# A decoder layer on one core: the normalized rows of the residual are made in the last pair's slot and kept in DRAM

## The chip, the cores and the metric

The kernel runs on one core of a Trainium2 chip. A core has five engines with a queue each: TensorE (PE) for matmuls, VectorE (DVE) and ScalarE (ACT) for elementwise work, GpSimd (POOL), and SyncE (SP), which here issues nearly all DMA transfers. PE writes its results to PSUM; everything else lies in SBUF, and the weights, the input and some scratch tensors lie in DRAM. Each engine works through its own instructions in an order that is fixed when the kernel is built. The metric is the time of the program on the device in microseconds.

## The reference

A hybrid decoder layer in float32, with 512 tokens, 16 learned meta tokens in front of them, and a width of 1024. Sliding-window attention and an RWKV-7 time mixing read the same normalized input, and their gated sum is projected and added to that same normalized input:

```python
h = layer_norm(jnp.concatenate([meta, x], axis=1), ln0_g, ln0_b)
proj = h @ w_in[l]
# q, k, v, zr, gate_att, gate_rwkv are cut out of proj
att = lax.map(lambda qkv: swa_one(...), (q, k, v))
rw = rwkv7_time_mix(zr, ...)
merged = jax.nn.sigmoid(gate_att) * att + jax.nn.sigmoid(gate_rwkv) * rw
h = layer_norm(ALPHA * h + merged @ w_out[l], ln1_g[l], ln1_b[l])
ff = jnp.square(jax.nn.relu(h @ w_ff1[l])) @ w_ff2[l]
h = layer_norm(ALPHA * h + ff, ln2_g[l], ln2_b[l])
```

The change concerns the `h` in `ALPHA * h + merged @ w_out[l]`: token rows of the input, normalized with `ln0_g` and `ln0_b`.

## The kernel before

**Precision.** Every float32 matmul is made of three matmuls of rounded parts: high by high, high by low, low by high. Each weight tile is therefore loaded (L268), cast to its high part on ACT (L258) and subtracted to its low part on DVE (L261). The tiles `wraw`, `whi` and `wlo` rotate in two to three buffers.

**Start.** The four blocks of 128 token rows are loaded, their mean and inverse deviation are computed and kept for the whole kernel in `moments0`, and the normalized rows are transposed to `hhi` and `hlo` (channels by tokens). The token rows themselves are not kept: their memory is given to the next stage.

**Pairs.** The 16 heads are worked on in 8 pairs, in slots. A slot weaves two things into PE's order: dense units (24 matmuls each with weights from `w_in`, later the output projection with `w_out`), and short steps of the attention and of the RWKV scan at given times within the slot. `weave` takes steps of a unit until the time of the next item is reached, then issues that item. This hand-written order holds for PE alone. The orders of DVE, ACT, POOL and SP come from a planner that starts what is ready by rank; `with ahead(n)` raises the rank of the instructions in it by n places, and a negative n lowers it.

In the last slot (`s == PAIRS`, about 563 to 604 us) the scan of pair 7 is solved: triangular blocks, folds (L866 on DVE to `WT`, L884 on DVE to `AX`), a chain of seven dependent steps (L937 on PE, then L895 on DVE and L897 on ACT, each writing half of `Z`), then outputs and a group norm. The dense units of this slot are the first three quarters of the output projection: L1244 to L1246, in four units of (half of the columns n, two token blocks), three quarters q of the input channels each. By then the sum of pairs 0 to 5 has come back from DRAM to the tiles `mf` in the buffers "u", "L", "tw", "ta", "Px", "rk" and was split to `hhi` and `hlo` by `merged` (L1211 on ACT, L1212 on DVE).

**Join.** After the slot the pools of the pairs are closed, and pools for the rest are opened in their memory. `res` holds the four blocks of token rows (128 x 1024 each). The rows are loaded again from `x` (L1443), and `ln0_g` and `ln0_b` are broadcast to 128 partitions (L1434, 512 KB each). Block 3 is normalized in four POOL passes (L1451); blocks 0, 1 and 2 in two DVE passes each (`norm_rows`, L1438 and L1439). Meanwhile PE does the last quarter of the output projection, block by block: twelve matmuls each. `first_norm(b)` then adds the projection to `res[b]` (L1501), takes statistics (L1482), normalizes (L1506, with L226 on POOL for the inverse root), turns the block on PE (L1512, eight transposes), applies `ln1_g` and `ln1_b` on ACT (L1515), and splits it to `h1hi` (L1520, ACT) and `h1lo` (L1521, DVE). The planner, not the hand-written order, places these instructions on PE.

**Feed-forward.** `up` (L331 to L333) multiplies by `w_ff1`, squares the positive part, and `project` multiplies by `w_ff2`. The first three tiles of `w_ff1` are applied to the first 256 tokens (blocks 0 and 1) before the other 256, so that PE can begin before blocks 2 and 3 are ready.

Of the kernel before, what the change touches and what calls it, by code (L numbers as in the profile page):

```python
# [11 lines left out]
F32 = mybir.dt.float32  # L12
# [3 lines left out]
ALU = mybir.AluOpType  # L16
# [4 lines left out]
P = 128  # L21
D = 1024
KT = D // P
SEQ = 512
# [6 lines left out]
NCH = SEQ // C  # L31
# [36 lines left out]
ROW0 = {}  # L68
# [11 lines left out]
SBB = 2  # L80
# [4 lines left out]
NBUF = {'AX': 2, 'BK': 1, 'NT': 2, 'GR': 2, 'Z': 8}  # L85
# [46 lines left out]
def hybrid_layer_kernel(ctx: ExitStack, tc: tile.TileContext, I: dict, out: bass.AP):  # L132
    nc = tc.nc
    dve, act, pool, pe = nc.vector, nc.scalar, nc.gpsimd, nc.tensor
# [8 lines left out]
    dr = ctx.enter_context(tc.tile_pool(name="dr", bufs=1, space=DRAM))  # L143

    @contextmanager
    def ahead(n):

        now = tc.cur_priority
        tc.cur_priority = now - n
        yield  # L150
        tc.cur_priority += n
# [22 lines left out]
    rows = xp.tile([NCOLS, P], F32, name="rows")  # L174
# [54 lines left out]
    def normalize(src, n, tag, on_act):  # L229

        st = xp.tile([P, 2, 6], F32, name="st" + tag)
        for q in range(2):
            dve.bn_stats(st[:n, q, :], src[:n, q * 512 : (q + 1) * 512])
        mv = cst.tile([P, 2], F32, name="mv" + tag)
        dve.bn_aggr(mv[:n], st[:n].rearrange("p a b -> p (a b)"))
        r = rstd_of(cst, mv, n, LN_EPS, tag)
        if on_act:
            nm = xp.tile([P, 2], F32, name="nm" + tag)
            dve.tensor_scalar(nm[:n, 0:1], mv[:n, 0:1], -1.0, None, op0=ALU.mult)
            act.activation(nm[:n, 1:2], nm[:n, 0:1], AF.Copy, scale=r[:n])  # L240
            act.activation(src[:n], src[:n], AF.Identity, bias=nm[:n, 1:2], scale=r[:n])
        else:
            dve.tensor_scalar(
                src[:n], src[:n], mv[:n, 0:1], r[:n], op0=ALU.subtract, op1=ALU.mult
            )
        return mv[:, 0:1], r

    moments0 = [normalize(xt[b], P, str(b), b < 2) for b in range(4)]
# [120 lines left out]
    def step():  # L369

        name, gen = units[0]
        t = next(gen, None)
        if t is None:
            units.pop(0)
            finished.add(name)
            return 0.0
        return t

    def weave(items, rest):


        t = 0.0
        for at_, need, what in sorted(items, key=lambda i: i[0]):
            while units and (t < at_ or not set(need) <= finished):
                t += step()
            assert set(need) <= finished
            what()
        while rest and units:
            step()
# [5 lines left out]
    at = p2.enter_context(tc.tile_pool(name="at", bufs=1))  # L395
    pew = ctx.enter_context(ExitStack())
    ew = pew.enter_context(tc.tile_pool(name="ew", bufs=1))
# [595 lines left out]
    A = {}  # L993
# [225 lines left out]
            nc.sync.dma_start(A["m", j], md[j])  # L1219


    acc = {}
    wout = {}
    bank = {}
    for n, pools in enumerate((((dn, "dn"), (pat, "a")), ((pg, "g"), (pch, None)))):
        for b in range(4):
            pool_, tag = pools[b // 2]
# [102 lines left out]
    F = partial  # L1330

    def scan(j):

        need = (f"k{j}", f"r{j}", f"v{j}")
        return [
            (0.0, need, F(rwkv_scores, j, 0)),
            (3.2, (), F(rwkv_meta, j)),
            (3.2, (), F(rwkv_scores, j, 1)),
            (3.2, (), F(rwkv_inverse, j)),
            (5.6, (), F(rwkv_bonus, j)),  # L1340
            (12.4, (), F(rwkv_turn_scores, j)),
            (19.0, (), F(rwkv_turn_keys, j)),
            (16.0, (), F(rwkv_inverse_place, j)),
            (21.4, (), F(rwkv_turn_values, j)),
        ]

    def solve(j):

        return [
            (0.0, (), F(rwkv_blocks, j, 0)),  # L1350
            (0.0, (), F(rwkv_start, j, 0)),
            (1.4, (), F(rwkv_blocks, j, 1)),
            (1.4, (), F(rwkv_start, j, 1)),
            (3.2, (), F(rwkv_blocks, j, 2)),
            (3.2, (), F(rwkv_start, j, 2)),
            (4.6, (), F(rwkv_blocks, j, 3)),
            (6.4, (), F(rwkv_turn_inverse, j)),
            (8.4, (), F(rwkv_fold, j, 0)),
            (10.6, (), F(rwkv_fold, j, 1)),
        ] + [(11.6 + 0.95 * c, (), F(rwkv_chain, j, c)) for c in range(NCH - 1)] + [  # L1360
            (18.6, (), F(rwkv_outputs, j)),
            (24.5, (), F(rwkv_norm, j)),
        ]

    def project_in(j):
        return [
            (0.0, (), F(rwkv_begin, j)),
            (5.6, (), F(rwkv_lora, j, 0)),
            (7.4, (), F(rwkv_lora, j, 1)),
            (20.4, (f"k{j}",), F(rwkv_sums, j)),  # L1370
        ]
# [13 lines left out]
    def join(j, t2):  # L1385
        return [(t2, (f"gr{j}",), F(merge, j))]

    with tc.manual_schedule(engines={mybir.EngineType.PE}):
        for s in range(-1, PAIRS + 1):
            if s <= PAIRS:  # L1390
                units[:] = [u for u in all_units[: marks[s + 1]] if u[0] not in finished]
            items = []
            if s > 0:
                items += solve(s - 1)
            if 0 <= s < PAIRS:
                items += scan(s)
            if s == -1:
                items += [
                    (0.0, (), F(rwkv_begin, 0)),
                    (9.0, ("wa",), F(rwkv_lora, 0, 0)),  # L1400
                    (10.4, (), F(rwkv_lora, 0, 1)),
                    (20.0, ("k0",), F(rwkv_sums, 0)),
                ]
            if 0 <= s < PAIRS - 1:
                items += project_in(s + 1)
            if s == 0:
                items += [(18.0, ("av",), F(aside_heads, 0))]
            if s == 4:
                items += [(26.0, (), F(aside_heads, 1))]
            if s in (1, 5):  # L1410
                items += [(8.6, (), turn_heads)]
            if 0 < s < PAIRS - 1:
                items += attend(s - 1) + join(s - 1, 31.5)
            if s == PAIRS - 1:
                items += [(10.0, (), merged_before)]
                items += attend(s - 1, t1=20.5) + join(s - 1, 26.5)
                items += attend(s, 16.5)[:4]
                items += [(27.2, (), F(load_out, q, 0)) for q in range(3)]
            if s == PAIRS:
                items += attend(s - 1, t1=1.0)[4:] + join(s - 1, 25.5)  # L1420
                items += [(2.0, (), F(merged, s - 2)), (25.6, (), F(merged, s - 1))]
            weave(items, True)
    pew.close()
    p2.close()
# [5 lines left out]

    def rowvec(name, pool_=rp, tag=None):
        t = pool_.tile([P, D], F32, name="rv" + name, tag=tag or "rv" + name[-1], bufs=WB[2] if tag else 1)
        src = I["rows"][ROW0[name] : ROW0[name] + KT].rearrange("(a r) p -> a (r p)", a=1)
        nc.sync.dma_start(t, src.to_broadcast([P, D]))  # L1434
        return t

    def norm_rows(t, mean, r, g_, b_):
        dve.scalar_tensor_tensor(t, t, mean, g_, op0=ALU.subtract, op1=ALU.mult)  # L1438
        dve.scalar_tensor_tensor(t, t, r, b_, op0=ALU.mult, op1=ALU.add)  # L1439

    res = [rp.tile([P, D], F32, name=f"res{b}") for b in range(4)]
    for b in range(4):
        nc.sync.dma_start(res[b], I["x"][b * P : (b + 1) * P, :])  # L1443
    g0, b0 = rowvec("ln0_g"), rowvec("ln0_b")

    mean, r = moments0[3]
    for op, t in zip(
        (ALU.subtract, ALU.mult, ALU.mult, ALU.add),
        (mean.to_broadcast([P, D]), g0, r.to_broadcast([P, D]), b0),
    ):  # L1450
        pool.tensor_tensor(res[3], res[3], t, op=op)  # L1451

    def project(k0, nk, xhi, xlo, n, hold=2, more=None):

# [68 lines left out]
            )  # L1523

    for b in range(4):
        if b < 2:
            norm_rows(res[b], *moments0[b], g0, b0)
        for n in range(2):
            for d in range(2):
                project_out(KT // 2 - 1, n, b, d)  # L1530
        if 0 < b <= NORMED:
            with ahead(400):
                first_norm(b - 1)
    norm_rows(res[2], *moments0[2], g0, b0)
    pps.close()
    pa = ctx.enter_context(tc.tile_pool(name="pa", bufs=1, space=PSUM))
    ffp = ctx.enter_context(tc.tile_pool(name="ffp", bufs=1))
# [10 lines left out]
    for half in range(2):  # L1548
# [34 lines left out]
        for f in range(split_f, NF):  # L1583
            up(f, load("w_ff1", half * NF + f), 0, SEQ, pb)
            if half == 0 and f in (6, 10):

                row = rowvec(("ln1_g", "ln1_b")[f // 10], wst, "wraw")
                for b in range(4):
                    dve.tensor_tensor(res[b], res[b], row, op=(ALU.mult, ALU.add)[f // 10])
        if half == 0:  # L1590
            g2, b2 = rowvec("ln2_g"), rowvec("ln2_b")
            st2 = stats_tiles()
        for n in range(2):
            ns = slice(n * 512, (n + 1) * 512)
            acc = project(half * NF, NF, fhi, flo, n, HOLD if half and n else 2, ffp)
            for b in range(4):
                dve.scalar_tensor_tensor(
                    res[b][:, ns], res[b][:, ns], 1.0 if half else ALPHA, acc[b],
                    op0=ALU.mult, op1=ALU.add,
# [58 lines left out]
```

## Time and profile before

| | |
|---|---|
| median of 3 runs | 1010.41 us (1008.91 to 1010.78) |
| the profiled execution | 1007.33 us |
| its span, first to last instruction | 1005.4 us |
| mean granted clock of TensorE | 0.985 |
| busy: PE, DVE, ACT, POOL | 948.8, 657.7, 469.9, 55.2 us |
| DMA | 101.26 MB, mean 101 GB/s |

The rows shown below are of one execution. Times within it count from the first instruction. In a row of the timeline the columns are start, length, engine, line, operation, output and inputs, shapes, count; in brackets stands how long the engine had been idle before it, and behind the arrow what ended that. Consecutive instructions of one kind are merged, with their count. In a row that groups instructions, the three numbers behind the count are the shortest, middle and longest duration in ns. "L331" is line 331 of the kernel; weights tiles of all stages go through the same lines L258, L261 and L268.

### The profile page before, as it was taken

Reading aid. Unit: us, or ns where it says so; the run is one execution under the profiler, and the core shown is the slowest. Engines: PE = TensorE matmul, PEld = TensorE weight load, DVE = VectorE, ACT = ScalarE, POOL = GpSimd, SP = SyncE. Lnnn points to the kernel's source line nnn. Section 1 sums busy time; section 2 is a strip of 40 time slices with the busy share of each in tenths; the row PEclk is TensorE's granted clock in tenths of the full one; section 3 lists DMA queues with packets and bytes.
Section 4 is the critical chain, followed back from the end, with each engine's and each line's share of the span. In section 5 each row is a group of like instructions: output and inputs, shape, how many; then the busy total and the mean of one; then the engine's idle time right before and its main releaser. Section 6 shows DMA issues by size and latency. Waiting matters only on the chain.

```text
span 1005.4 us, 19165 instructions
## 1 busy us (share of the span) xinstructions
PE 948.8 (94%) x7533; PEld 792.4 (79%) x7533; DVE 657.7 (65%) x1493; ACT 469.9 (47%) x1238; POOL 55.2 (5%) x112
## 2 busy tenths in 40 slices
PE   4999899999999999999999998699999999999996
PEld 3989688787888878888777676688888888888885
DVE  8678687887886878878786548866432234443436
ACT  6536457574574655845537622644332223432220
POOL 2000000010000100001000004100000000000001
PEclk9999999999999999999999999799999999999999
DMA  7454433224333333242433114323322333232232
GB/s 267 93 148 117 94 88 106 73 69 111 89 91 97 93 106 72 63 131 70 126 90 80 54 64 167 126 95 116 105 84 84 108 101 104 85 105 89 79 105 83
DMA packets 80369, 101.26 MB, mean 101 GB/s; under 512 B 47510, under 2 KB 54408, under 8 KB 80280
## 3 DMA queue, kind: packets, MB, share of 16 engines
q1 hardware_dynamic: 78784, 97.97, 33.3%
q10 hardware_dynamic: 1496, 2.08, 0.6%
q8 instruction: 59, 0.97, 0.4%
q14 instruction: 30, 0.25, 0.1%
HBM read 84.19 MB, written 11.64 MB: 95 GB/s over the span
## 4 chain that ended last, share of the span: by engine, by line
PE 67%; DVE 17%; ACT 9%; issue 3%; DMA 2%; SPq 0%; POOL 0%; DVEq 0%; ACTq 0%; POOLq 0%
PE dps L331 12%; PE dps L332 11%; PE dps L333 11%; PE acc L1465 6%; PE acc L1467 6%; PE acc L1466 6%; ACT Z L744 2%; DVE wlo L261 2%; PE sc L659 2%; PE av L1180 2%; DVE ftmp L764 1%; DVE AX L884 1%; DVE Xf L768 1%; PE o L1244 1%; ACT whi L258 1%
## 5 line engine op out<-in xcount | busy, mean ns | idle before, releaser
L258 ACT CAST whi<-wraw 128x512 fp32r<-128x512 f32 x242 | 141.8, 618 | 281.8 <-PE dps L332 135.5
L261 DVE TENSOR_TENSOR wlo<-wraw,whi 128x512 fp32r<-128x512 f32 x242 | 159.6, 685 | 172.0 <-ACT whi L258 171.5
L331 PE MATMUL dps<-hhi,whi 128*128 128x264 f32 (+1 forms) x640 | 219.8, 343 | 1.8 <-ACT whi L258 1.1
L332 PE MATMUL dps<-hlo,whi 128*128 128x264 f32 (+1 forms) x640 | 205.4, 321 | 1.0 <-DVE hlo L312 1.0
L333 PE MATMUL dps<-hhi,wlo 128*128 128x264 f32 (+1 forms) x640 | 204.5, 320 | 0.4 <-DVE wlo L261 0.4
L331 PEld LDWEIGHTS dps<-hhi,whi 128*128 128x128 f32 x640 | 122.3, 191 | 15.3 <-issue 1.4
L333 PEld LDWEIGHTS dps<-hhi,wlo 128*128 128x128 f32 x640 | 121.8, 190 | 9.3 <-DVE wlo L261 0.6
L332 PEld LDWEIGHTS dps<-hlo,whi 128*128 128x128 f32 x640 | 122.2, 191 | 6.2 <-DVE hlo L312 1.8
L331 PE MATMUL dps<-h1hi,whi 128*128 128x512 f32 (+1 forms) x264 | 100.1, 380 | 5.7 <-ACT h1f L1515 3.7
L332 PE MATMUL dps<-h1lo,whi 128*128 128x512 f32 (+1 forms) x264 | 99.9, 379 | 0.2 <-DVE h1lo L1521 0.2
L333 PE MATMUL dps<-h1hi,wlo 128*128 128x512 f32 (+1 forms) x264 | 99.9, 379 | 0.0
L331 PEld LDWEIGHTS dps<-h1hi,whi 128*128 128x128 f32 x264 | 50.4, 191 | 15.4 <-ACT h1f L1515 4.1
L332 PEld LDWEIGHTS dps<-h1lo,whi 128*128 128x128 f32 x264 | 50.3, 191 | 9.3 <-DVE h1lo L1521 0.4
L333 PEld LDWEIGHTS dps<-h1hi,wlo 128*128 128x128 f32 x264 | 50.3, 191 | 9.1
L1465 PE MATMUL acc<-whi,hhi 128*128 128x512 f32 x128 | 50.7, 396 | 0.0
L1467 PE MATMUL acc<-whi,hlo 128*128 128x512 f32 x128 | 50.4, 394 | 0.0
L1466 PE MATMUL acc<-wlo,hhi 128*128 128x512 f32 x128 | 50.0, 391 | 0.0
L1465 PE MATMUL acc<-whi,fhi 128*128 128x512 f32 x112 | 43.6, 389 | 0.0
L1466 PE MATMUL acc<-wlo,fhi 128*128 128x512 f32 x112 | 43.6, 389 | 0.0
L1467 PE MATMUL acc<-whi,flo 128*128 128x512 f32 x112 | 43.6, 389 | 0.0
L897 ACT ACTIVATE Z<-ch,PC 64x64 f32<-64x64 f32 x56 | 17.3, 310 | 44.9 <-DVE Z L895 43.6
L744 ACT COPY Z<-vt 64x64 f32<-64x64 f32 x128 | 26.5, 207 | 9.0 <-PE vt L737 7.6
(296 smaller groups left out, 1738.3 us busy)
## 6 DMA issues: line engine op xcount, KB each, us to landing
wraw<-in_w_ff_dram SPq DMA_DIRECT2D x64, 512.0 KB, 3.5
wraw<-in_w_in_dram SPq DMA_DIRECT2D x52, 512.0 KB, 4.0
wraw<-in_w_out_dram SPq DMA_DIRECT2D x8, 512.0 KB, 3.7
xt<-in_x_dram SPq DMA_DIRECT2D x4, 512.0 KB
Nd<-NT SPq DMA_DIRECT2D x16, 128.0 KB, 2.9
bv<-bv SPq DMA_DIRECT2D x8, 256.0 KB
bvm<-bv SPq DMA_DIRECT2D x8, 256.0 KB, 3.4
qs<-qhi SPq DMA_DIRECT2D x16, 128.0 KB, 3.4
```

The costliest lines, as they stand in the source:

```text
L258: act.copy(hi[:n, qs], raw[:n, qs])
L261: dve.tensor_tensor(lo[:n, qs], raw[:n, qs], hi[:n, qs].bitcast(F32), op=ALU.subtract)
L331: pe.matmul(ps, whi, xhi, start=first, stop=False)
L332: pe.matmul(ps, whi, xlo, start=False, stop=False)
L333: pe.matmul(ps, wlo, xhi, start=False, stop=last)
L659: pe.matmul(scs[e][:, c * P : (c + 1) * P], BK[ER[e], 4 * i + c, :], AXg[ER[e], e, 4 * i + c], start=True, stop=True,)
L744: act.copy(Z[2 * i + cc][64 * (1 - e) : 64 * (1 - e) + 64, e, :], vt[64 * cc : 64 * cc + 64, i * P + e * HD : i * P + (e + 1) * HD],)
L897: act.activation(dst, src[ER[e]], AF.Copy, scale=scale)
L1180: pe.matmul(av[64 * e : 64 * e + 64, (2 * i + n) * P : (2 * i + n + 1) * P], vs[:, 2 * i + n], ps[:, 2 * n + e, :], start=(d == 0), stop=( ...
L1465: pe.matmul(acc[b], xhi[k][:, bs], hi[:, ws], start=first, stop=False)
L1466: pe.matmul(acc[b], xhi[k][:, bs], lo[:, ws], start=False, stop=False)
L1467: pe.matmul(acc[b], xlo[k][:, bs], hi[:, ws], start=False, stop=last)
```

## The change

The normalization of the residual's rows moves from the join to the last pair's slot. Three time units into that slot `residual_gain` broadcasts `ln0_g` into the buffer of `BK` and `ln0_b` into one of the two buffers of `sb`. At 3, 6, 9 and 12 units `residual_rows(b)` takes block b in two halves of 512 columns: each half is loaded from `x` into a buffer of the pairs' pool that is free by then, normalized in place by two DVE passes that are ranked 300 places back, and stored to the new DRAM tensor `rd`. At the join `res[b]` is loaded from `rd[b]`; the two broadcasts, the four POOL passes and the six DVE passes that stood there are gone. `rowvec` now calls the shared `broadcast`; the rows for the later norms are made as before.

```diff
+    rd = dr.tile([4, P, D], F32, name="rd")
+
+    def broadcast(t, name):
+        src = I["rows"][ROW0[name] : ROW0[name] + KT].rearrange("(a r) p -> a (r p)", a=1)
+        nc.sync.dma_start(t, src.to_broadcast([P, D]))
+        return t
+
+    def residual_gain():
+        g_ = ew.tile([P, NCH, P], F32, name="g0", tag="BK", bufs=NBUF["BK"])
+        b_ = at.tile([P, 4, 2, P], F32, name="b0", tag="sb", bufs=SBB)
+        A["g0"] = broadcast(g_.rearrange("p a c -> p (a c)"), "ln0_g")
+        A["b0"] = broadcast(b_.rearrange("p n e s -> p (n e s)"), "ln0_b")
+
+    def residual_rows(b):
+
+        mean, r = moments0[b]
+        for q in range(2):
+            qs = slice(q * SEQ, (q + 1) * SEQ)
+            tag = (("u", "L"), ("tw", "ta"), ("Px", "rk"), ("v", "rkh"))[b][q]
+            t = ew.tile([P, SEQ], F32, name="h0", tag=tag)
+            nc.sync.dma_start(t, I["x"][b * P : (b + 1) * P, qs])
+            with ahead(-300):
+                for scalar, row, ops in (
+                    (mean, "g0", (ALU.subtract, ALU.mult)), (r, "b0", (ALU.mult, ALU.add))
+                ):
+                    dve.scalar_tensor_tensor(t, t, scalar, A[row][:, qs], op0=ops[0], op1=ops[1])
+            nc.sync.dma_start(rd[b, :, qs], t)
...
+                items += [(3.0, (), residual_gain)]
+                items += [(3.0 + 3 * b, (), F(residual_rows, b)) for b in range(4)]
...
     res = [rp.tile([P, D], F32, name=f"res{b}") for b in range(4)]
     for b in range(4):
-        nc.sync.dma_start(res[b], I["x"][b * P : (b + 1) * P, :])
-    g0, b0 = rowvec("ln0_g"), rowvec("ln0_b")
-
-    mean, r = moments0[3]
-    for op, t in zip(
-        (ALU.subtract, ALU.mult, ALU.mult, ALU.add),
-        (mean.to_broadcast([P, D]), g0, r.to_broadcast([P, D]), b0),
-    ):
-        pool.tensor_tensor(res[3], res[3], t, op=op)
+        nc.sync.dma_start(res[b], rd[b])
...
     for b in range(4):
-        if b < 2:
-            norm_rows(res[b], *moments0[b], g0, b0)
         for n in range(2):
             for d in range(2):
                 project_out(KT // 2 - 1, n, b, d)
         if 0 < b <= NORMED:
             with ahead(400):
                 first_norm(b - 1)
-    norm_rows(res[2], *moments0[2], g0, b0)
```

More of the change, by code (lines that the diff above doesn't have):

```diff
@@ L1432, in rowvec @@
         t = pool_.tile([P, D], F32, name="rv" + name, tag=tag or "rv" + name[-1], bufs=WB[2] if tag else 1)
-        src = I["rows"][ROW0[name] : ROW0[name] + KT].rearrange("(a r) p -> a (r p)", a=1)
-        nc.sync.dma_start(t, src.to_broadcast([P, D]))
-        return t
+        return broadcast(t, name)
     def norm_rows(t, mean, r, g_, b_):
```

## The prediction

> **What bounds the kernel now.** I read the page's busy shares first, then the stretches around the join, then the chain that ended last there, and last the rows of the engines in time. TensorE is the bound nearly everywhere, so a microsecond is won only where TensorE stands still or is clocked down.
>
> ```profile
> PE 948.8 (94%) x7533; PEld 792.4 (79%) x7533; DVE 657.7 (65%) x1493; ACT 469.9 (47%) x1238; POOL 55.2 (5%) x112
> ```
>
> The stretches are cut at events of this trace: the last pair's slot, the join up to the last quarter of the output projection, that quarter, and the first norm with the first half-width matmuls of the feed-forward in two parts. Columns: stretch, length, busy time and count of PE, PEld, DVE, ACT, POOL, then granted clock, DMA share, GB/s.
>
> ```profile
> 563.30:604.00 40.70, 40.41 (x387) 29.73 (x387) 15.26 (x30) 12.06 (x33) 1.63 (x1) 0.96 0.18 64
> 604.00:613.40 9.40, 8.63 (x37) 7.07 (x38) 5.36 (x8) 3.63 (x6) 0.97 (x1) 1.00 0.88 309
> 613.40:624.60 11.20, 11.11 (x48) 8.64 (x46) 11.03 (x4) 2.29 (x4) 10.23 (x4) 1.00 0.28 115
> 624.60:639.70 15.10, 3.94 (x16) 3.14 (x16) 14.43 (x26) 7.92 (x21) 1.50 (x2) 0.66 0.30 98
> 639.70:654.50 14.80, 12.45 (x88) 11.96 (x88) 11.85 (x25) 9.64 (x25) 1.35 (x2) 0.88 0.35 114
> 654.50:680.00 25.50, 25.26 (x144) 22.26 (x145) 17.02 (x26) 11.15 (x24) 0.00 (x0) 1.00 0.31 104
> ```
>
> Up to 624.6 us PE is full; between 624.6 and 654.5 it is busy 16.39 of 29.9 us, at granted clocks of 0.66 and 0.88; after 654.5 it is full again. So the hole holds 13.5 us of idle time, and some more of slow clock. VectorE is the full engine in front of the hole. The chain that ended last says why (start, length, what):
>
> ```profile
> 605.71 7.76 DMA rvln_g<-in_rows_dram
> 613.57 1.22 DVE res L1438
> 614.79 0.55 issue
> 615.35 3.43 DVE res L1438
> 618.77 2.89 DVE res L1439 x2
> 621.66 3.21 issue
> 624.87 1.27 DVE res L1501 x2
> ```
>
> The rows' gain vector lands at 613.5, then four residual passes hold VectorE until 624.9, and only then L1501 adds the projection (its accumulators are long done). Two of the passes take 3.4 us instead of 1.28, in the same time as the four POOL passes:
>
> ```profile
> 614.42 3.27 POOL L1451 TENSOR_TENSOR res<-res,rvln_g 128x1024 f32<-128x1024 f32 x1
> L1438 DVE SCALAR_TENSOR_TENSOR res<-res,mv,rvln_g x3: 1280/1847/3427, 613.6 to 635.1; 128x1024 f32<-128x1024 f32 x3
> L1439 DVE SCALAR_TENSOR_TENSOR res<-res,rs,rvln_b x3: 1279/2908/3421, 618.7 to 636.9; 128x1024 f32<-128x1024 f32 x3
> ```
>
> PE's own rows show what the late norm costs: the waits in brackets, and the transposes at 1.97 us for eight while the clock is down against 1.09 later.
>
> ```profile
> 624.11 0.40 PE L1246 MATMUL o<-whi,hlo 128*128 128x512 f32 x1
> 630.25 1.97 PE L1512 MATMUL tp<-con,res 128*128 128x128 f32 x8 [5.74 <-DVE res L1506]
> 634.05 1.97 PE L1512 MATMUL tp<-con,res 128*128 128x128 f32 x8 [1.83 <-DVE res L1506]
> 639.72 0.58 PE L331 MATMUL dps<-h1hi,whi 128*128 128x256 f32 x1 [3.70 <-ACT h1f L1515]
> 650.74 1.09 PE L1512 MATMUL tp<-con,res 128*128 128x128 f32 x8 [0.37 <-DVE res L1506]
> 654.52 0.51 PE L331 MATMUL dps<-h1hi,whi 128*128 128x256 f32 x2 [1.98 <-ACT h1hi L1520]
> ```
>
> **Part 1, the join.** The change takes from it the two broadcasts, the two passes each of rows 0, 1 and 2 on DVE, and the four POOL passes (3.27 us the longest shown). The four loads of `res` stay, with another source, at the same place of SP's queue, so row 0 is there within a few us of 604: the stretch to 613.4 moved 309 GB/s, so 0.52 MB takes 1.7 us, and the four 6.8 us. The 1 MB of broadcast goes (3.4 us of DMA), but nothing then waits for the weights behind it.
>
> What is late next is the accumulator. PE's last 48 matmuls start 0.233 us apart and finish at 624.5, so they begin at 613.3, and each token block takes 2.8 us: block 0 is complete at 616.3, block 1 at 619.1. The norm of a block from there, by these rows:
>
> ```profile
> 624.87 1.27 DVE L1501 SCALAR_TENSOR_TENSOR res<-res,o 128x512 f32<-128x512 f32 x2
> L1482 DVE BATCH_NORM_STATS2 fst<-res x16: 667/690/695, 626.1 to 998.5; 128x6 f32<-128x512 f32 x16
> 628.79 0.56 POOL L226 TENSOR_TENSOR rsf<-rsf,mhalf 128x1 f32<-128x1 f32 x1 [4.93 <-DVE rsf L225]
> 629.38 0.81 DVE L1506 TENSOR_SCALAR res<-res,fmv,rsf 128x1024 f32<-128x1024 f32 x1
> ```
>
> The first half's add and statistics lie under the second half's matmuls; behind the last matmul stand 0.65 + 0.69, then some 0.3 for two tiny instructions, 0.6 on POOL, 0.81 on DVE: about 3.2 us. So block 0 can be turned at 619.5 instead of 630.25, and block 1 at 622.3.
>
> Now ScalarE sets the pace. In the present run it works through blocks 0 and 1 as follows:
>
> ```profile
> 631.40 1.86 ACT L1515 ACTIVATE h1f<-tp,vc 128x128 f32<-128x128 f32 x5 [7.11 <-PE tp L1512]
> 633.13 0.63 ACT L1520 CAST h1hi<-h1f 128x512 fp32r<-128x512 f32 x1
> 638.14 1.53 ACT L1515 ACTIVATE h1f<-tp,vc 128x128 f32<-128x128 f32 x4
> 644.19 0.28 PE L331 MATMUL dps<-h1hi,whi 128*128 128x256 f32 x1
> 644.31 0.28 PE L332 MATMUL dps<-h1lo,whi 128*128 128x256 f32 x1
> ```
>
> The first feed-forward matmul follows the last scaling of block 1 (639.67, then 639.72). From 631.4 to 639.67 it is 8.3 us; five scalings take 1.86, so 0.37 each, and the sixteen 5.9. The other 2.4 are four casts (three of these blocks, one half of a weight), 0.6 each: 8 x 0.37 + 2 x 0.6 = 4.2 us a block. PE's work between that start and the second half-width pass (654.52) is three groups of 24 matmuls 0.12 us apart, 8.6 us, and sixteen transposes, 2.2 us, plus 1.7 us for the slow clock that followed the idle 3.70.
>
> How early the sixteen transposes of blocks 0 and 1 stand in PE's order I cannot see, since behind the slot the order is the planner's. So three cases:
> - both among the last 48 matmuls: ACT starts half a group of transposes behind 619.5, at 620.1, is through block 0 at 624.3, does two weight casts (1.2) and ends the scalings of block 1 (8 x 0.37 + 0.6 = 3.6) at 629.1. PE, done at 624.5 + 2.2 = 626.7, waits 2.4 us only; 629.1 + 8.6 + 2.2 = 639.9 for the second pass, 14.6 us earlier than 654.5.
> - block 0 among them, block 1 behind them: PE is through the 48 at 625.6 and through block 1 at 626.7; ACT has block 1 from 626.2 to 630.4 (3.6 and half a weight, 0.6). PE has waited 3.7 us, as long as the 3.70 that was followed by a slow clock, so I charge 1.7: 630.4 + 8.6 + 1.7 + 2.2 = 642.9, gain 11.6.
> - both behind: ACT runs from 625.1, its 8.3 us end at 633.4, 633.4 + 12.5 = 645.9, gain 8.6.
>
> I take the middle, 11.6, with 8.6 and 14.6 as ends. Behind 654.5 PE is full in both, so the gain stays to the end.
>
> The clock in these cases is read from rows alone. [...]
>
> **Part 2, the slot of the last pair.** Added there: 16 DVE passes of 512 columns, on SP 2 broadcasts, 8 loads and 8 stores.
>
> ```profile
> L1438 DVE SCALAR_TENSOR_TENSOR res<-res,fmv,rvln_g x8: 740/743/747, 983.2 to 1000.2; 128x512 f32<-128x512 f32 x8
> 575.40 0.69 DVE L1186 SCALAR_TENSOR_TENSOR ga<-ga,av 128x512 f32<-128x512 f32 x1 [3.28 <-PE av L1180]
> 581.23 1.28 DVE L884 TENSOR_TENSOR AX<-AX,gq 128x512 f32<-128x512 f32 x2 [2.48 <-PE gq L879]
> 587.71 0.28 DVE L895 TENSOR_SCALAR Z<-ch,PC 64x64 f32<-64x64 f32 x1 [0.85 <-PE ch L937]
> L895 DVE TENSOR_SCALAR Z<-ch,PC x7: 269/275/278, 586.6 to 595.1; 64x64 f32<-64x64 f32 x7
> ```
>
> 16 x 0.743 = 11.9 us on an engine that idles 40.70 - 15.26 = 25.4 us there; POOL does nothing beside them but 1.63 us, so they run at the uncontended length. Idle pieces like 3.28 and 2.48 us hold three or four passes each. The cost is only what a pass, once begun, keeps an urgent instruction waiting. Floor: 0. Ceiling: the seven chain steps L895, whose result PE needs at once, each late by a whole pass, 7 x 0.74 = 5.2. The passes ask for a lower rank (300 back) and their rows come early in the slot, while the chain runs from 586 to 595; a gap of 0.85 even takes one pass unharmed. So I take 1.2, the floor's side.
>
> SP and DMA: 18 issues at some 0.33 us are 6 us of a queue with five weight loads to issue in the slot.
>
> ```profile
> L268 SPq DMA_DIRECT2D wraw<-in_w_out_dram x5: 327/328/333, 561.8 to 594.9; - x5
> 583.53 1.14 ACT L258 CAST whi<-wraw 128x512 fp32r<-128x512 f32 x2 [10.01 <-PE o L1246]
> wraw<-in_w_out_dram SPq DMA_DIRECT2D x8, 512.0 KB, 3.7
> ```
>
> The first of the five is cast only at 583.5, some 20 us after it was asked for, with 3.7 us to landing: a store that waits for DVE in front of a weight load is covered. If that cover is gone, the load is late by as much as DVE is. 1 MB of broadcast, 2 of loads and 2 of stores are 17 us at 309 GB/s in a stretch of 40.7 that uses 0.18 of the DMA. The wait of the four `res` loads on the stores costs nothing as long as the stores end before 603.9. I charge nothing for these.
>
> **The sum.** 11.6 - 1.2 = 10.4 us less. The profiled execution took 1007.33 (span 1005.4), which gives 996.9; the median of the runs is 1010.41, 3.1 above it, so the forecast of a median is 1010.4 - 10.4 = 1000.0. A change within 0.2% (2 us) could not be told from none, as the three runs themselves lie 1.9 apart.
>
> **Rivals.**
> - *ACT and a slow clock keep most of the hole.* Transposes behind the last matmul (8.6), a slot cost of 3 to 5 as the seven chain steps take half to a whole pass: 8.6 - 4 = 4.6 less, 1006. For it: in the present order not one transpose stands among the last 48 matmuls. Against: there the norm was late (L1501 at 624.87), which by itself put them behind.
> - *Slower: DVE stands in the slot behind a load.* Its order is fixed when the kernel is built. If the passes of a half row are placed as if its load had come, DVE waits for the landing with all behind it, the fold and the chain among it. Eight half rows, each held 3.5 us (a row of the DMA list shows 3.7) plus 1.5 of passes, are 40 us against 25.4 of idle time: 14.6 late, less 11.6: 3 us slower, 1013. It decides once the holds add up to more than 25.4 - 11.9 + 11.6 = 25 us, 3.1 a half row. For it: the chain shows DVE held by a broadcast until 613.5. Against: eight tiles of their own and the slot's idle DMA let the loads run far ahead.
> - *The change does not do what it says.* The low-ranked passes slip to the end of the slot, the stores end behind 604, and `res` row 0 is there only near 622, some 6 us behind its accumulator. 11.6 - 6 = 5.6 is left, and the passes, crowded among the chain steps, take their ceiling of 5.2: 1010. For it: the rank is low. Against: DVE's 25.4 idle us lie all along the slot.
>
> **Chances.** Forecast (995 to 1003) 0.57; small gain (1003 to 1008) 0.19; no change 0.06; slower 0.18. Faster by over 0.2%: 0.57 + 0.19 = 0.76. The range of 994.5 to 1009 takes in the first two and part of the third, from 14.6 at no slot cost (995.8, and 1 below for the runs' scatter) to nearly none; the forecast's own range is 995 to 1003.
>
> **What would show it.** Right: no residual pass on DVE or POOL between 604 and 640, L1501 near 615, the first transposes before or at 625, the first feed-forward matmul near 630, the granted clock of that stretch above 0.8, and in the slot PE still busy for all but a microsecond or two. Wrong: bracketed DMA waits on the new passes, PE waiting for L895, L866 or L884 in the slot, `res` landing after 616, or a wait of PE for ACT's scalings as long as now.

## The result, and the profile after

| | before | after |
|---|---|---|
| median | 1009.66 us (1008.62 to 1010.78, 4 runs) | 997.45 us (995.2 to 997.59, 4 runs) |
| the profiled execution, its span | 1007.33 us, 1005.4 us | 997.59 us, 995.8 us |
| mean granted clock | 0.985 | 0.988 |

The ratio is 0.9871, with a 95% interval of 0.9852 to 0.989: 12.2 us less between the medians, where 10.4 less and a time of 1000.0 had been forecast. In the changed kernel the lines behind the new functions are numbered 21 to 29 higher: L1501 is now L1522, L1506 L1527, L1512 L1533, L1515 L1536. The new passes are L1247, their stores L1248.

The page's busy shares of after:

```profile
PE 946.2 (95%) x7533; PEld 790.8 (79%) x7533; DVE 654.3 (66%) x1503; ACT 469.6 (47%) x1238; POOL 43.4 (4%) x108
```

POOL lost the four passes (12 us of busy time); VectorE, with ten instructions more, has nearly the sum it had. So the gain is, in the main, not less work but work elsewhere.

Two traces are set beside each other by an event that both have. I use the gated output of the last slot, on ScalarE, and call its start z; here it is in before and then in after:

```profile
603.93 0.78 ACT L975 ACTIVATE z<-yt,vc 128x512 f32<-128x512 f32 x1 [5.62 <-PE yt L969]
```

```profile
606.02 0.78 ACT L975 ACTIVATE z<-yt,vc 128x512 f32<-128x512 f32 x1 [5.62 <-PE yt L969]
```

This execution of after is 2.1 us later at z, though hardly anything was gained or lost in the slot; where that comes from is told at the end. Times are therefore given as distances from z. The stretches of after, in the columns of the prediction (stretch, length, PE, PEld, DVE, ACT, POOL, clock, DMA share, GB/s):

```profile
563.30:606.10 42.80, 41.09 (x390) 30.00 (x390) 25.69 (x47) 14.46 (x40) 1.63 (x1) 0.96 0.35 117
...
615.50:626.70 11.20, 11.20 (x54) 9.18 (x53) 9.95 (x20) 4.00 (x9) 1.11 (x2) 1.00 0.44 155
626.70:632.10 5.40, 1.76 (x12) 1.14 (x10) 5.31 (x10) 5.40 (x16) 0.00 (x0) 0.89 0.29 97
632.10:644.90 12.80, 12.62 (x86) 12.62 (x87) 8.59 (x19) 10.41 (x27) 1.48 (x2) 0.78 0.26 84
644.90:680.00 35.10, 35.07 (x191) 30.44 (x190) 22.26 (x34) 15.58 (x32) 0.00 (x0) 1.00 0.30 100
```

The hole of 29.9 us that held 13.5 us of idle time is now 18.2 us (626.7 to 644.9) with 3.8 of idle time. VectorE is still busy for 9.95 of the 11.2 us from 615.5 to 626.7, but on the norms and on splitting weights, not on the rows. PE's own rows of after:

```profile
624.35 1.03 PE L1533 MATMUL tp<-con,res 128*128 128x128 f32 x8
627.37 1.09 PE L1533 MATMUL tp<-con,res 128*128 128x128 f32 x8
632.28 0.58 PE L331 MATMUL dps<-h1hi,whi 128*128 128x256 f32 x1 [3.81 <-ACT h1f L1536]
635.86 1.91 PE L1533 MATMUL tp<-con,res 128*128 128x128 f32 x8
641.48 1.03 PE L1533 MATMUL tp<-con,res 128*128 128x128 f32 x8
645.23 0.28 PE L331 MATMUL dps<-h1hi,whi 128*128 128x256 f32 x1
```

Before there were five waits here, three of transposes and two of the feed-forward, 13.6 us in all; one is left, 3.81. The first feed-forward matmul stands at z + 26.3 (before: 639.72, z + 35.8), the second half-width pass at z + 39.2 (before: 654.52, z + 50.6): 11.4 us earlier. From there to the end of the span it is 350.6 us after and 350.9 before. The chain that ended last in after goes through ScalarE alone at this place (start, length, what):

```profile
624.51 0.45 PE tp L1533 x4
624.98 1.85 ACT h1f L1536 x5
...
```

It ends in the matmul at 632.28, and VectorE is no longer on it. Its rows between the end of the slot and there:

```profile
616.88 0.69 DVE L1522 SCALAR_TENSOR_TENSOR res<-res,o 128x512 f32<-128x512 f32 x1
...
618.69 0.67 DVE L1522 SCALAR_TENSOR_TENSOR res<-res,o 128x512 f32<-128x512 f32 x1
...
622.45 0.69 DVE L1522 SCALAR_TENSOR_TENSOR res<-res,o 128x512 f32<-128x512 f32 x1 [0.18 <-PE o L1275]
623.09 0.81 DVE L1527 TENSOR_SCALAR res<-res,fmv,rsf 128x1024 f32<-128x1024 f32 x1
```

In the slot, between the group norms of pairs 6 and 7 (POOL's L960, the same instructions in both), the stretch of before and then that of after, in the columns as above:

```profile
541.88:599.39 57.51, 54.43 (x543) 40.15 (x543) 29.13 (x57) 30.66 (x95) 1.64 (x2) 0.97 0.16 54
```

```profile
544.19:601.48 57.29, 54.18 (x543) 40.02 (x543) 39.13 (x73) 30.75 (x95) 1.63 (x2) 0.97 0.43 141
```

Sixteen passes more (57 to 73 instructions on DVE) and 87 GB/s more, at the same granted clock of 0.97, and the stretch is no longer. The last pass runs at 579.87 and the eight stores are issued by 581; the loads of `res` follow 25 us later (SP's rows, then the row of the DMA list with the time to landing in us):

```profile
566.41 14.55 SPq L1248 DMA_DIRECT2D rd<-h  x8
...
606.00 2.01 SPq L1472 DMA_DIRECT2D res<-rd  x4
```

```profile
res<-rd SPq DMA_DIRECT2D x4, 512.0 KB, 6.1
```

### The profile page after: what moved, and what is told of

Its sections match the earlier page's. It is cut to its first block, busy times and chain, and to the rows that moved or that the text cites. A ratio compares the mean times of both kernels' runs of the same rounds, so it can differ in the third digit from the quotient of the medians.

```text
span 995.8 us, 19206 instructions
## 1 busy us (share of the span) xinstructions
PE 946.2 (95%) x7533; PEld 790.8 (79%) x7533; DVE 654.3 (66%) x1503; ACT 469.6 (47%) x1238; POOL 43.4 (4%) x108
## 4 chain that ended last, share of the span: by engine, by line
PE 69%; DVE 17%; ACT 8%; issue 2%; DMA 2%; SPq 0%; POOL 0%; DVEq 0%; ACTq 0%; POOLq 0%
PE dps L331 12%; PE dps L332 11%; PE dps L333 11%; PE acc L1486 6%; PE acc L1488 6%; PE acc L1487 6%; DVE wlo L261 2%; ACT Z L744 2%; PE sc L659 2%; PE o L1273 2%; PE av L1180 2%; DVE AX L884 2%; PE o L1275 1%; PE o L1274 1%; DVE Xf L768 1%
```

## The experiments

Each kernel was compared with runs of the kernel before on its own chip. "Second pass" is the second half-width pass of the feed-forward, as a distance from z: 50.6 us before, 39.2 after.

### Only the slot's part

Before, with the broadcasts, loads, passes and stores of the slot added, and the join left as it was: nobody reads `rd`.

```diff
...
+                items += [(3.0, (), residual_gain)]
+                items += [(3.0 + 3 * b, (), F(residual_rows, b)) for b in range(4)]
...
```

> The slot's part alone: rows are made and stored in the last pair's slot as in the change, but the join loads and normalizes the residual as before (the stored rows are not read). Theory (all of the gain is made at the join, and the slot's passes run in idle time of VectorE): as before within 2 us, 1008 to 1011, and the join's stretch as before. Rival (the passes delay the slot's chain): 1011 to 1015, with TensorE waiting for L895, L866 or L884. Second rival (part of the gain comes from the new order of VectorE in the slots, where the changed kernel's landmarks come 1.1 us closer together than before): 1006 to 1008.5.

Measured: 1011.04 us (1006.92 to 1015.21, 10 runs) against 1009.86, ratio 1.0008 (0.9987 to 1.0029). The median lies on the edge between the theory and the first rival. All of the gain is made at the join, and the slot's price is, by the interval, between 1.3 us less and 2.9 us more than nothing. In this kernel's profile the stretch between the two group norms is 3 us longer than in before and after:

```profile
540.64:600.93 60.29, 57.20 (x543) 42.31 (x543) 39.26 (x73) 30.79 (x95) 1.63 (x1) 0.92 0.39 134
```

PE's idle time in it is the same 3.1 us as in both (57.51 - 54.43, 57.29 - 54.18, 60.29 - 57.20); what differs is the granted clock, 0.92 against 0.97. So PE does not wait for the passes, as the first rival had it; the clock is told of in the last section.

### The passes doubled

The change, with a third instruction behind each of the two, the maximum of the tile with itself. It leaves the values as they are: 32 instructions of 512 columns in the slot instead of 16.

```diff
                     dve.scalar_tensor_tensor(t, t, scalar, A[row][:, qs], op0=ops[0], op1=ops[1])
+                    dve.tensor_tensor(t, t, t, op=ALU.max)
```

> The changed kernel with 32 passes in the slot instead of 16: behind each of them one that takes the maximum of the tile with itself (0.69 us, the values stay). 23 us of passes stand against some 25 us of VectorE's idle time. Theory (idle time hides passes of low rank until they reach the chain of the slot): 1 to 5 us more than the changed kernel, 998.5 to 1002.5. Rival (at this rank they go wherever room is, at no cost): within 1 us, 996.5 to 998.5. Second rival (the stores come late and the join waits for them): over 1003.

Measured: 995.69 us (995.52 to 996.62, 4 runs), ratio 0.9865 (0.9839 to 0.9892). The stretch between the group norms:

```profile
543.23:600.07 56.84, 52.98 (x543) 39.27 (x543) 48.23 (x89) 30.92 (x95) 1.63 (x1) 1.00 0.43 143
```

VectorE is busy 48.2 of 56.8 us and the slot is not longer than in after. My theory of a small price for each pass falls; ranked 300 back, they cost nothing that the medians show, even twice. This profile had a granted clock of 1.00 in the slot, though; the second profile of the change, shown in the last section, had that too and a slot of 56.22 us, so a price of some 0.6 us for the doubling is not excluded.

### The rank turned round

The change, with the passes ranked ahead instead of back.

```diff
-            with ahead(-300):
+            with ahead(600):
```

> The changed kernel, with the 16 passes of the slot ranked 600 places ahead instead of 300 behind. Theory (VectorE has idle time enough, so the rank costs little): the changed kernel's time and up to 2 us more, 997 to 999.5. Rival (the rank is what protects the slot): the passes hold up what TensorE waits for, by up to 5.2 us: 1000 to 1003.

Measured: 1004.41 us (1003.04 to 1006.37, 6 runs), ratio 0.9939 (0.9917 to 0.9962): above both ranges, about 7 us of the gain are gone. They went in one place, and it is not the chain of seven steps where I had put the ceiling. VectorE's rows at the start of the slot (the softmax of the last pair is L1147 and L1148), then ScalarE's and PE's behind them:

```profile
564.65 0.75 DVE L1247 SCALAR_TENSOR_TENSOR h<-h,mv,g 128x512 f32<-128x512 f32 x1 [0.52 <-DMA h<-in_x_dram]
...
567.25 1.41 DVE L1247 SCALAR_TENSOR_TENSOR h<-h,rs,b 128x512 f32<-128x512 f32 x2
568.58 0.16 DVE L1147 TENSOR_TENSOR sm<-sm,es 128x8 f32<-128x8 f32 x1
569.25 0.19 DVE L1148 RECIPROCAL sm<-sm 128x8 f32<-128x8 f32 x1
```

```profile
569.54 2.44 ACT L1150 ACTIVATE sb<-sb,sm 128x128 f32<-128x128 f32 x8 [4.54 <-DVE sm L1148]
```

```profile
572.01 1.09 PE L1160 MATMUL pt<-con,sb 128*128 128x128 f32 x4 [8.48 <-ACT sb L1150]
```

In after PE waits 2.00 us for the same scaling, here 8.48. Between 558 and 568.6 us twelve of the passes run ahead of two instructions of 0.16 and 0.19 us. The slot is 64.5 us long (544.83 to 609.34 between the group norms), 7.2 more than in after: 6.5 of waiting, and 0.7 of PE's busy time at a clock of 0.92 against 0.97. From z to the end of the span it takes 390.0 us against 389.8 in after. The wait for a load that the slower rival needed appears here too, 0.52 us of it, once.

### The passes of row 3 off POOL

Before, with block 3 normalized by two passes on DVE behind those of block 2, and nothing on POOL.

```diff
-    mean, r = moments0[3]
-    for op, t in zip(
-        (ALU.subtract, ALU.mult, ALU.mult, ALU.add),
-        (mean.to_broadcast([P, D]), g0, r.to_broadcast([P, D]), b0),
-    ):
-        pool.tensor_tensor(res[3], res[3], t, op=op)
...
     norm_rows(res[2], *moments0[2], g0, b0)
+    norm_rows(res[3], *moments0[3], g0, b0)
```

> The kernel before, but block 3 of the residual is normalized by two VectorE passes behind those of block 2, not by four GpSimd passes. Theory (the four passes in front of L1501 are what holds the norm, 11.3 us with GpSimd beside them and 5.1 without): L1501 begins some 6 us earlier, at about 619, less the 2.6 us that two more passes take in front of blocks 2 and 3: 1004 to 1006.5. Rival (what holds the norm is the landing of the broadcast at 613.5): no gain beyond 1 us, 1008.5 to 1010.

Measured: 1006.46 us (1004.14 to 1008.74, 10 runs), ratio 0.9961 (0.9946 to 0.9977). Its four passes ahead of the add, and PE's waits:

```profile
611.87 2.48 DVE L1438 SCALAR_TENSOR_TENSOR res<-res,mv,rvln_g 128x1024 f32<-128x1024 f32 x2 [1.05 <-DMA rvln_g<-in_rows_dram]
614.26 2.48 DVE L1439 SCALAR_TENSOR_TENSOR res<-res,rs,rvln_b 128x1024 f32<-128x1024 f32 x2
616.66 1.28 DVE L1494 SCALAR_TENSOR_TENSOR res<-res,o 128x512 f32<-128x512 f32 x2
```

```profile
625.93 1.42 PE L1505 MATMUL tp<-con,res 128*128 128x128 f32 x8 [2.31 <-DVE res L1499]
...
646.78 1.77 PE L1505 MATMUL tp<-con,res 128*128 128x128 f32 x8 [3.41 <-DVE res L1499]
```

Four passes take 4.8 us instead of 11.3: 1.8 to 3.4 us each beside POOL, 1.2 to 1.3 alone. So the longest passes beside POOL, 3.4 us, are some 2 us longer than the 1.28 they take alone; what holds them up, no row shows. The 6.5 us saved in front of the first add reach the first feed-forward matmul (z + 29.0, before z + 35.8), but only 2.6 are left at the second pass (z + 48.0): block 3's two passes now stand on DVE in front of the norms of blocks 2 and 3, and PE waits 3.41 there, at a granted clock of 0.77 between the two points against 0.88 in before.

### The broadcasts first

Before, with the two broadcasts issued ahead of the four loads of rows.

```diff
+    g0, b0 = rowvec("ln0_g"), rowvec("ln0_b")
     for b in range(4):
         nc.sync.dma_start(res[b], I["x"][b * P : (b + 1) * P, :])
-    g0, b0 = rowvec("ln0_g"), rowvec("ln0_b")
```

> The kernel before, but the two broadcasts are issued ahead of the four loads of the rows. Theory (both the late landing and the passes stand in front of L1501): the gain vector is there by 607 or 608, the passes begin near 610 instead of 613.6 and the first of them run before GpSimd starts: 4 to 6 us earlier, 1004 to 1006. Rival (the contention with GpSimd alone): L1501 at most 1 to 2 us earlier, 1007.5 to 1009. Second rival (the landing alone, passes as slow as before): 3 to 4 us earlier, 1005.5 to 1007.

Measured: 1006.2 us (1003.67 to 1007.09, 8 runs), ratio 0.996 (0.9942 to 0.9978), just above what I had given it, and within the second rival's range. The adds of block 0 now start at z + 11.7, nearly as early as in after (z + 10.9), and yet the second pass is at z + 48.65. VectorE's rows, then PE's:

```profile
619.10 3.01 DVE L1439 SCALAR_TENSOR_TENSOR res<-res,rs,rvln_b 128x1024 f32<-128x1024 f32 x1
...
627.16 0.81 DVE L1506 TENSOR_SCALAR res<-res,fmv,rsf 128x1024 f32<-128x1024 f32 x1 [2.09 <-POOL rsf L226]
```

```profile
628.02 1.97 PE L1512 MATMUL tp<-con,res 128*128 128x128 f32 x8 [4.98 <-DVE res L1506]
```

The contention with POOL moved to a later pass, and the tiny inverse root of block 0 (L226, at 626.57) stands on POOL behind the four passes there. So of the 9 us won in front of the first add 1.9 are left at the second pass, and 3.7 between the medians, while the passes are where they were.

### Both

The edits of the last two together.

```diff
+    g0, b0 = rowvec("ln0_g"), rowvec("ln0_b")
     for b in range(4):
         nc.sync.dma_start(res[b], I["x"][b * P : (b + 1) * P, :])
-    g0, b0 = rowvec("ln0_g"), rowvec("ln0_b")
-
-    mean, r = moments0[3]
...
     norm_rows(res[2], *moments0[2], g0, b0)
+    norm_rows(res[3], *moments0[3], g0, b0)
```

> The kernel before with both edits at once: block 3 on VectorE, and the broadcasts issued first. Apart they gave 1006.5 and 1006.2 against 1009.9. Theory (the passes stand in front of L1501, and once that begins near 616 the accumulators hold it, as in the changed kernel; but the four passes of blocks 2 and 3, 5.1 us, stay on VectorE while it splits and norms): 1002 to 1005, some 5 to 8 us above the changed kernel. Rival (only what stands in front of L1501 counts): nearly all of the gain, 998 to 1000.5. Second rival (both edits take away the same stall): 1005 to 1006.5.

Measured: 1006.13 us (1002.7 to 1010.49, 10 runs), ratio 0.9964 (0.9945 to 0.9983): no better than either, in the range of the second rival. Both edits take away the same stall: the adds of block 0 start at z + 11.7, as with the broadcasts first alone. VectorE's rows, then PE's:

```profile
624.82 1.27 DVE L1438 SCALAR_TENSOR_TENSOR res<-res,mv,rvln_g 128x1024 f32<-128x1024 f32 x1
...
629.67 0.81 DVE L1499 TENSOR_SCALAR res<-res,fmv,rsf 128x1024 f32<-128x1024 f32 x1 [0.45 <-POOL rsf L226]
```

```profile
630.54 1.97 PE L1505 MATMUL tp<-con,res 128*128 128x128 f32 x8 [4.37 <-DVE res L1499]
```

With the landing early and POOL empty, the passes of the later rows stand among the norms of the earlier ones: block 1 is normalized at z + 24.9 here (629.67) and at z + 20.5 in after. From the first add to the first feed-forward matmul (z + 30.4) VectorE is busy 18.0 of 18.7 us. The late landing and the contention, the two causes that the chain of before names, are worth 4 us together; the other 7 go with the passes themselves, which keep their place on a full VectorE: 4.1 of them are lost by that matmul, and 3.2 behind it, where PE idles 3.0 us up to the second pass.

### Half of the rows

The change, with blocks 0 and 1 from the slot, and blocks 2 and 3 loaded from `x` and normalized on DVE at the join.

```diff
-                items += [(3.0 + 3 * b, (), F(residual_rows, b)) for b in range(4)]
+                items += [(3.0 + 3 * b, (), F(residual_rows, b)) for b in range(2)]
...
-        nc.sync.dma_start(res[b], rd[b])
+        nc.sync.dma_start(res[b], rd[b] if b < 2 else I["x"][b * P : (b + 1) * P, :])
+    g0, b0 = rowvec("ln0_g"), rowvec("ln0_b")
...
+    for b in (2, 3):
+        norm_rows(res[b], *moments0[b], g0, b0)
```

> Half of the change: blocks 0 and 1 are made in the slot; blocks 2 and 3 are loaded from the input and normalized by VectorE at the join, behind the first two blocks, with the broadcasts there again. Theory (the passes of blocks 2 and 3 also cost, since VectorE is full between the first transposes and the second half-width pass): 2 to 4 us above the changed kernel, 999.5 to 1001.5. Rival (only the passes in front of L1501 count): 997 to 999.

Measured: 999.81 us (997.09 to 1002.2, 4 runs), ratio 0.9902 (0.9872 to 0.9933). PE's rows:

```profile
627.88 1.59 PE L1534 MATMUL tp<-con,res 128*128 128x128 f32 x8 [1.88 <-DVE res L1528]
632.36 0.58 PE L331 MATMUL dps<-h1hi,whi 128*128 128x256 f32 x1 [2.89 <-ACT h1f L1537]
...
648.52 0.58 PE L331 MATMUL dps<-h1hi,whi 128*128 128x256 f32 x2 [2.02 <-ACT h1hi L1542]
```

The second pass stands at z + 43.9, between the two kernels; the four passes of some 1.28 us that are left at the join cost 4.7 us at that point. By the first feed-forward matmul (z + 27.8) it is 1.5 us, since the passes delay the norms that are needed first; the other 3.2 are lost behind it, where PE idles 2.6 us for the late blocks 2 and 3. So the rows that are needed last also matter.

### What is left: twelve matmuls as cover

The one wait left in after is PE's 3.81 us for ScalarE. Twelve matmuls of the third quarter of the output projection (blocks 2 and 3, half n = 1) were taken out of the slot and put behind the last quarter of block 1. So blocks 0 and 1 are complete 2.8 us earlier, and PE still has work while their norms and scalings run.

```diff
                 for b in blocks:
+                    if (q, n, blocks) == (2, 1, (2, 3)):
+                        continue
                     project_out(q, n, b, d)
...
     for b in range(4):
+        if b == 2:
+            for d in range(2):
+                for c in (2, 3):
+                    project_out(2, 1, c, d)
```

> The changed kernel, with twelve matmuls of the output projection (third quarter, second half of the columns, blocks 2 and 3; 2.8 us) taken out of the slot's last unit and put behind block 1's last quarter. The work is the same. Theory (what is left of the hole is TensorE's wait of 3.8 us for ScalarE's scalings and the slow clock behind it, 1.7 us): blocks 0 and 1 are complete 2.8 us earlier, the first feed-forward matmul comes 2 to 3 us earlier, and with a wait under 2 us the clock stays up: 992.5 to 995.5. Rival (ScalarE and the weight casts, whose buffers come free later, set the pace): 996.5 to 999.

Measured: 993.6 us (992.96 to 996.07, 4 runs), ratio 0.9846 (0.982 to 0.9872). Since the step is small, it was run again on one chip with the change:

> The change itself once more, on the same chip as the next kernel. Both theories: 995 to 998 us, ratio to before about 0.987.

> The kernel with twelve output matmuls moved behind block 1's last quarter, on the same chip as the change. Theory (the wait of 3.8 us and the slow clock behind it at the join are taken away, block 0's and block 1's transposes both stand ahead of the last output matmuls): 2 to 4 us below the change on this chip. Rival (the 2.1 us between the two second passes is scatter of two executions): within 1 us of the change.

Measured: the change 998.08 us (995.04 to 999.14, 5 runs; ratio 0.9878, 0.9854 to 0.9901), this version 995.88 us (994.47 to 997.02, 4 runs; ratio 0.9854, 0.9829 to 0.9878). The medians are 2.2 us apart, though the two intervals overlap. The second run's stretches from the first add of block 0 to the first feed-forward matmul and from there to the second pass, and PE's transposes:

```profile
616.70:631.03 14.33, 13.86 (x70) 10.99 (x68) 11.84 (x23) 7.83 (x21) 1.12 (x2) 1.00 0.31 115
631.03:644.39 13.36, 11.12 (x90) 10.50 (x89) 11.31 (x24) 10.79 (x27) 1.10 (x2) 1.00 0.38 119
```

```profile
622.56 1.04 PE L1535 MATMUL tp<-con,res 128*128 128x128 f32 x8
625.00 1.09 PE L1535 MATMUL tp<-con,res 128*128 128x128 f32 x8 [0.47 <-DVE res L1529]
```

Both blocks are turned while output matmuls are left, there is no wait in front of the feed-forward, and the clock stays at 1.00. The second pass stands at z + 36.3 (z = 608.13); at z + 37.1 in the first run; the change's was at z + 39.2 and, in its second profile, at z + 38.8. So each profile of this version is 1.7 to 2.9 us better at that point than each of the change, as expected, and by its ratios the version is the fastest kernel here; a gain over the change of 2 us is what the medians say, not what their intervals prove.

## Why the prediction was right

- **What bounds the join.** Right. The passes on VectorE were the cause, and neither the late landing nor the contention by itself: taking away both leaves 7 of the 11 us in place.
- **The three cases.** Right, the middle one: block 0's transposes stand among the last output matmuls, block 1's behind them. Predicted and measured as distances from z: first feed-forward matmul 26.5 and 26.3, PE's wait 3.7 and 3.81, from there to the second pass 12.5 and 12.95, second pass 39.0 and 39.2. The gain there was put at 11.6 and is 11.4. The slow clock that I charged behind the 3.7 us came in both profiles of the change (0.79 and 0.86 up to the second pass). In before the clock was already down when its 3.70 us began (transposes of 1.97 us), so that row alone could not price such a wait; after, where the transposes ahead of it take 1.03 and 1.09, can. The first rival, which needed both blocks turned behind the last matmul, falls. That it was the middle case was a choice between two ends, not a derivation, and in that lucky; and none of the cases mentions the waits of 0.37 and 1.98 us in before's 14.8 us, which each of them leaves out. They did go away: in after PE is busy throughout the 12.95 us.
- **The norm of a block.** Wrong in size. I had 3.2 us from the last matmul of block 0 to its turning; from its second add (618.69) alone to the transposes (624.35) it is 5.7, since both adds and a statistics pass of block 1 and the first add of block 2 stand in between on VectorE (the row at 622.45 is the last of these). It did not show in the end, as a second error went the other way: ScalarE then had both blocks in one stretch, without a weight cast among them, and took 7.2 us for them (624.98 to 632.22, the end of the last scaling), where the middle case had 10.3, a gap included. That these two cancel to 0.2 us is luck.
- **The slot.** The term that looks too large. I charged 1.2 us; the stretch is 0.2 shorter than before, and twice the passes give no more in the medians. The slot's part alone gives 0.8 more by its ratio, with an interval that reaches from -1.3 to 2.9, and so excludes neither 0 nor 1.2. The ceiling of 5.2 was wrong in place and in size: if the passes run too early, PE waits 6.5 us longer for the softmax at the start of the slot, and the slot is 7.2 us longer, while the chain steps lose nothing. My sentence that the rows come while the chain is not yet running holds (the last pass is at 579.87).
- **SP, the stores and the DMA.** Right at nothing: the stores are issued 25 us before the loads that read them, and the loads land some 6 us behind their issue, ahead of the first add at 616.88. With that the third rival falls. None of the sixteen passes waits for a load in after, so the second falls too.
- **The sum.** 11.4 at the join, 0.3 behind it and 0.2 in the slot are 11.9 us, beside 12.2 between the medians. The forecast of 10.4 was 0.2 too high at the join, charged 1.4 too much in the slot and left out the 0.3 behind.
- **What would show it.** No pass between 604 and 640: so. L1522 at 616.88, 614.8 when the 2.1 us of offset are taken off; the transposes at 624.35; the feed-forward at 630.2 without the offset. PE idles 1.7 us in the slot's stretch, but 1.4 of these belong to the wait for the softmax (564.73), which in before lay just ahead of the stretch. The clock was to be above 0.8: 0.89 and then 0.78, so it missed by a little in the second part. One sign of being wrong did appear: PE waits for ACT's scalings as long as before, 3.81 us and 3.70. It was badly chosen, since the middle case itself has 3.7 there.

## What to carry to other kernels

When a profile shows a late landing and a contention in front of a full engine, remove them one at a time before believing that they are the cause: here both together gave a third of what moving the work gave. Work that is not urgent cost nothing that the medians show when it was ranked behind all else, even on an engine 85% busy, and 7 us in the same slot when it was ranked ahead; so ask what short urgent instruction it could stand in front of, not how many microseconds it takes. And when a change leaves one wait behind, a few independent matmuls held back for that place can cover it: here that was worth some 2 us, by the medians, for a wait of 3.8.

## What the runs showed of the hardware

**The same wait is followed by different clocks.** At the start of the slot PE waits about 2 us for the softmax. The stretches of 4 us that begin with the end of that wait, in the two profiles of the one changed kernel, the first after a wait of 2.00 us, the second after one of 1.96 (the number behind POOL's is the granted clock):

```profile
564.73:568.73 4.00, 4.00 (x77) 2.56 (x78) 3.97 (x8) 3.92 (x13) 0.00 (x0) 0.67 0.77 194
568.73:572.73 4.00, 4.00 (x63) 3.12 (x62) 3.16 (x6) 1.54 (x6) 0.00 (x0) 0.91 0.53 207
```

```profile
563.58:567.58 4.00, 4.00 (x81) 2.72 (x81) 3.97 (x8) 3.91 (x13) 0.00 (x0) 1.00 0.72 203
567.58:571.58 4.00, 4.00 (x63) 3.19 (x62) 3.54 (x7) 2.03 (x6) 0.00 (x0) 1.00 0.65 249
```

And the second such stretch in the kernel with only the slot's part, whose wait was 1.98 us:

```profile
565.17:569.17 4.00, 4.00 (x44) 2.78 (x45) 1.83 (x4) 1.17 (x6) 0.00 (x0) 0.50 0.49 180
```

In these 4 us, at half the clock, PE gets through 44 matmuls, where the second 4 us of the other two have 63. The slot's length goes with it. Between the two group norms PE's busy time for the same 543 matmuls is 57.20 us in that kernel at a granted 0.92, 54.18 in after at 0.97, and 53.14 in the second profile of the change at 1.00:

```profile
543.03:599.25 56.22, 53.14 (x543) 39.40 (x543) 39.04 (x73) 30.66 (x95) 1.64 (x1) 1.00 0.44 144
```

So the 3 us by which the slot was longer with the slot's part alone are the clock's. All this contradicts what I read from one row of before, where 1.98 us of waiting was followed by a granted 1.00 (654.50 to 680.00), and took into the expectation of the version with the twelve matmuls, that a wait under 2 us leaves the clock alone: it may or may not. So it is with the 3.8 us wait of the join: from the first feed-forward matmul to the second pass the clock was 0.79 in one profile of the change and 0.86 in the other, 12.95 and 12.57 us. Executions of one order come out differently (0.67 and 1.00 behind waits of 2.00 and 1.96 us); what makes the difference, no run here shows.

**The same order of instructions takes up to 4.9 us more or less in its first 160 us.** All these kernels have the same order of instructions in that time, yet the first group norm on POOL starts at 153.24 us in before and at 158.15 in the last run above, and part of such an offset lasts: in after that norm starts at 157.72, and 2.1 us of the 4.5 are left at z. Here are the two rows, of before and of that run:

```profile
153.24 1.65 POOL L960 TENSOR_TENSOR grs<-grs,mhalf 128x8 f32<-128x8 f32 x1 [6.87 <-DVE grs L959]
```

```profile
158.15 1.65 POOL L960 TENSOR_TENSOR grs<-grs,mhalf 128x8 f32<-128x8 f32 x1 [6.88 <-DVE grs L959]
```

An effect of 2 us can therefore be read from distances within a trace and from medians of several runs, but not from two spans. The granted clock has a share in it: up to that norm it is 0.98 in before, 0.97 in after and 0.96 in the last run, and PE's busy time for the same matmuls 132.06, 133.71 and 135.00 us, so 2.9 of the 4.9 us are slower matmuls and 2.0 are waits. And from 480 to 500 us it is 0.91 in before and 1.00 in after, which is where after makes up part of its offset. What sets the clock and the rest stays open.
